# A two-layer attention kernel: whole-tile work moved from GpSimd to VectorE

## The chip, the cores and the metric

The kernel runs on one core of one Trainium2 chip. A core has five engines, each with an instruction queue of its own that it works through in order: TensorE (PE in the profile; its weight loads are listed as PEld), VectorE (DVE), ScalarE (ACT), GpSimd (POOL) and SyncE (SP, which here issues the DMA transfers). The metric is the device time of one launch in microseconds (us), the median of several runs.

## What is computed

Two layers are applied to 256 context tokens and to 1024 latent tokens of width 1024. Both layers norm the tokens, modulate them with a scale and a shift from a conditioning vector, mix the tokens with gated attention, project, norm again and add the result to the stream. Layer 0 uses differential attention (two softmaxes per head, subtracted), layer 1 multi-head latent attention. Cut to what matters:

```python
for i in range(2):
    hc = rmsnorm(x_ctx, g_pre[i]) * (1.0 + sc_c) + sh_c
    hl = rmsnorm(x_lat, g_pre[i]) * (1.0 + sc_l) + sh_l
    if i == 0:                       # 8 heads, q and k in two parts of 64, v of 128
        qc, kc, vc, gc = diff_project(hc, da_w_in[0])
        oc = diff_attend(qc, kc, vc, gc, lam, lam_init, da_g_sub[0])
        ql, kl, vl, gl = diff_project(hl, da_w_in[0])
        ql, kl = apply_rope(ql, *rope_da), apply_rope(kl, *rope_da)
        ol = diff_attend(ql, concat(kl, cache_k), concat(vl, cache_v), gl, ...)
    else:                            # 8 heads on a compressed latent of 256, 64 rotated dims
        qc, ckv_c, kpe_c, gc = mla_project(hc, ...)
        oc = mla_attend(qc, ckv_c, kpe_c, gc, mla_w_kvb[0])
        ql, ckv_l, kpe_l, gl = mla_project(hl, ...)
        ql, kpe_l = mla_rope(ql, kpe_l, *rope_mla)
        ol = mla_attend(ql, concat(ckv_l, cache_ckv), concat(kpe_l, cache_kpe), gl, mla_w_kvb[0])
    x_ctx = x_ctx + gt_c * rmsnorm(oc @ w_out[i], g_post[i])
    x_lat = x_lat + gt_l * rmsnorm(ol @ w_out[i], g_post[i])
# diff_attend: w = softmax(q0 k0) - lam * softmax(q1 k1); o = rmsnorm(w v) * g_sub * 0.2; o * silu(gate)
```

The outputs are both streams and the context tokens' keys, values and latents.

## The kernel before, in words

**Tiling.** Tokens are handled in five pairs of 128-row tiles, four latent pairs (0 to 3) and one context pair (4). Matrix products keep nearly full float32 precision by splitting each operand into a rounded high part and the low rest: `mm3` (L324) issues three matmuls for each product, high by high (L327), high by low (L328) and low by high (L329). So every operand needs a cast (the high part, mostly on ACT) and a subtraction (the low part).

**Where the low parts are made.** `weights` (L304) loads a weight tile `wst` by DMA, casts it on ACT to `wh` (L319) and subtracts to `wl` (L320): on GpSimd, or, where the caller gives `lo_engs=self.LO`, in turn on GpSimd and VectorE. `weights_x` (L347) does the same for the rotated weights on GpSimd (L365). `norm_pair_to_hT` (L280) transposes the normed tokens on PE (L290), applies scale and shift on ACT into `hfull` (L297; three buffers in layer 0, two in layer 1), casts to `hh` on VectorE (L298) and subtracts to `hl` (L299), on VectorE for some of the eight columns and on GpSimd for the others. `yT_load` (L1401) reloads layer 1's head outputs, casts them on ACT (L1407) and subtracts on GpSimd (L1408).

**Stages in order.**
1. Start (0 to about 100 us): modulation vectors, norm of layer 0, the first value projection. `norm_pair` (L256) takes the sums of squares on ACT (L263), adds them (L266), and `rstd` (L248) makes the reciprocal root on GpSimd in two steps (L251 scales and adds epsilon, L253 raises to the power -0.5); VectorE then scales the rows (L270).
2. Queries and keys of layer 0 (to about 330 us), `l0_qk_item` (L374): 32 x 3 matmuls for a half tile, an ACT copy (L421), a rotation in six steps (L427 twice, L428 twice, L429, L430) on GpSimd for queries and on VectorE for keys, then a split into high and low (L385, L386) and a store. Cached and context keys are rearranged on GpSimd (L406, L455).
3. Layer 0's attention (to about 970 us), `l0_heads` (L820): 72 units, nine per head. Each has scores on PE (L603), maxima on VectorE (L605, L612 to L614), exponentials on ACT (L617, L619), the weighted difference on VectorE (L648), transposes on PE (L671), their split on ACT and VectorE (L673, L674), and values on PE. Between these steps a feeder doles out the other projections (values, gates, modulation). After each pair of units `l0_values` (L678) norms the head's output: squares on ACT (L701), `rstd` on GpSimd, then, on GpSimd too, the factor `of` (L706) and the product (L707), and a store to DRAM. `y_chunk` (L743) reloads four heads' outputs two by two with the gate, multiplies them on GpSimd (L757), and PE transposes them (L768).
4. The seam (about 950 to 1150 us): `out_items` (L929) multiplies by the output weights, `residual` (L974) makes the post-norm and adds it to the stream (roots L983 and additions L989, L993 on GpSimd, the rest on VectorE), and layer 1's norm and transposes follow for each pair.
5. Layer 1's projections (to about 1340 us), its attention (`l1_heads` L1332, to about 1870 us) and its output projection with the residual again. Its attention has scores (L1277 to L1281), maxima (L1287, L1289), exponentials (L1295, L1296) and a scaling by the reciprocal sum (L1302).

**What sets the order.** The kernel's text gives a dependency graph and a priority; the framework then draws each engine's queue from it by an estimate of when each operand is ready. Only a stretch of PE at the start is ordered by hand. An engine's queue is therefore not in the order of the text, but once drawn it is fixed: an instruction whose operand is late holds all behind it.

**Buffers around the change.** `wh` and `wl` have five buffers, `wst` three; `ztmp` in `residual` has one; PSUM tiles of the scores have two.

## Time and profile before

| what | us |
|---|---|
| median of 3 runs | 1993.41 (1992.21 to 1994.4) |
| the profiled execution | 1997.65 |
| its span, first to last instruction | 1995.8 |
| granted TensorE clock over the span | 0.989 |

The profile is of one execution. Its page lists busy time of each engine, groups of instructions by line, and for each group what ended the idle time in front of it. "L320 POOL" is line 320 run on GpSimd. `wl<-wst,wh` is output and inputs by the program's tile names. A row of the waits reads "engine, tile and line that waited <- engine, tile and line that released it: us in total, times, longest". In a timeline a row is start, duration, engine, line, operation, and in brackets the idle time before it.

The page's forty slices of 50 us, each digit a busy share in tenths, show the stages:

```
PE   6999999999999999999998999999999999999998
DVE  4644446788878786888427533446667767777413
ACT  4422123667666665666435533335445554455421
POOL 3354443213121212224334442100000000004214
```

PE is nearly full from start to end, VectorE fullest in the two attentions, and GpSimd has work mainly in the first 1200 us and in the last 200.

### The profile page before, as it was taken

To read this page: it belongs to the slowest core of one execution; us is meant where nothing else is said; L and a number is where in the kernel's file an instruction comes from. 1 tells how busy PE (TensorE), PEld (TensorE's weight loads), DVE (VectorE), ACT (ScalarE), POOL (GpSimd) and SP (SyncE) were. 2 spreads that over 40 slices of the span, in tenths; PEclk is the share of its full clock that TensorE was granted. 3 is DMA by queue.
4 is the path that set the end of the run, shared out by engine and by line. 5 is a ranking of instruction groups with operands and counts; after the bars stand their busy time and mean duration, and the time that the engine had idled before them with its cause. 6 is when DMAs were issued, how large, how long until landed. Compare 5 with 4: busy or idle time off the path is not lost.

```text
span 1995.8 us, 36154 instructions
## 1 busy us (share of the span) xinstructions
PE 1911.7 (96%) x13468; PEld 1721.9 (86%) x13468; DVE 1248.4 (63%) x2461; ACT 963.9 (48%) x2409; POOL 498.9 (25%) x693
## 2 busy tenths in 40 slices
PE   6999999999999999999998999999999999999998
PEld 5788888798989787988898999889899999998998
DVE  4644446788878786888427533446667767777413
ACT  4422123667666665666435533335445554455421
POOL 3354443213121212224334442100000000004214
PEclk9999999999999999999998999999999999999999
DMA  8555544544455454455624312442110111113412
GB/s 307 170 169 175 188 157 137 157 138 132 128 147 162 129 165 127 133 148 180 194 98 135 97 51 62 145 135 60 42 36 28 47 39 50 38 38 96 160 56 106
DMA packets 225009, 237.66 MB, mean 119 GB/s; under 512 B 25313, under 2 KB 192577, under 8 KB 224705
## 3 DMA queue, kind: packets, MB, share of 16 engines
q1 hardware_dynamic: 224672, 235.29, 38.3%
q8 instruction: 107, 1.75, 0.4%
q14 instruction: 70, 0.57, 0.1%
q10 hardware_dynamic: 160, 0.05, 0.0%
HBM read 160.48 MB, written 74.78 MB: 118 GB/s over the span
## 4 chain that ended last, share of the span: by engine, by line
PE 43%; DVE 5%; POOL 3%; ACT 2%; issue 2%; DMA 2%; SPq 0%; POOLq 0%; ACTq 0%; DVEq 0%
PE pj L327 7%; PE pj L329 7%; PE pj L328 7%; PE tp L671 3%; PE tp L327 3%; PE tp L328 3%; PE tp L329 3%; PE S L1280 1%; PE S L1281 1%; PE S L1278 1%; PE S L1279 1%; PE S L1277 1%; PE S L603 1%; DVE ptl L674 1%; DMA yst<-yTd 1%
## 5 line engine op out<-in xcount | busy, mean ns | idle before, releaser
L327 PE MATMUL pj<-wh,hh 128*128 128x256 f32 (+1 forms) x1264 | 369.4, 292 | 6.6 <-DVE ptl L674 3.5
L328 PE MATMUL pj<-wl,hh 128*128 128x256 f32 (+1 forms) x1264 | 359.1, 284 | 6.1 <-DVE wl L320 3.7
L329 PE MATMUL pj<-wh,hl 128*128 128x256 f32 (+1 forms) x1264 | 358.8, 284 | 3.4 <-POOL hl L299 1.7
L320 POOL TENSOR_TENSOR wl<-wst,wh 128x512 fp32r<-128x512 f32 (+3 forms) x95 | 110.7, 1173 | 655.1 <-ACT wh L319 608.9
L327 PEld LDWEIGHTS pj<-wh,hh 128*128 128x128 f32 x1264 | 241.7, 191 | 11.7 <-DVE ptl L674 4.1
L328 PEld LDWEIGHTS pj<-wl,hh 128*128 128x128 f32 x1264 | 242.2, 192 | 8.3 <-DVE wl L320 4.1
L329 PEld LDWEIGHTS pj<-wh,hl 128*128 128x128 f32 x1264 | 241.7, 191 | 6.5 <-POOL hl L299 3.1
L329 PE MATMUL pj<-hh,wl 128*128 128x512 f32 (+1 forms) x512 | 188.5, 368 | 1.0 <-POOL wl L365 0.9
L327 PE MATMUL pj<-hh,wh 128*128 128x512 f32 (+1 forms) x512 | 188.3, 368 | 0.0
L328 PE MATMUL pj<-hl,wh 128*128 128x512 f32 (+1 forms) x512 | 187.8, 367 | 0.0
L605 DVE TENSOR_REDUCE mA<-S 128x1 f32<-128x1024 f32 x128 | 155.4, 1219 | 46.8 <-PE S L603 45.9
L617 ACT ACTIVATE e<-S,bias 128x1024 f32<-128x1024 f32 x128 | 142.9, 1117 | 81.6 <-DVE bias L614 81.4
L603 PE MATMUL S<-kl,q 128*128 128x512 f32 x512 | 150.4, 414 | 5.5 <-ACT e L617 5.1
L673 ACT CAST pth<-tp 128x512 fp32r<-128x512 f32 (+1 forms) x208 | 98.4, 511 | 83.0 <-PE tp L671 81.9
L673 ACT CAST pth<-pj 128x512 fp32r<-128x512 f32 (+1 forms) x192 | 98.4, 519 | 73.4 <-PE pj L671 70.8
L674 DVE TENSOR_TENSOR ptl<-tp,pth 128x512 fp32r<-128x512 f32 (+1 forms) x208 | 115.1, 580 | 14.1 <-ACT pth L673 13.3
L648 DVE SCALAR_TENSOR_TENSOR e<-e,cf,e 128x512 f32<-128x512 f32 (+1 forms) x192 | 121.4, 674 | 1.1
L674 DVE TENSOR_TENSOR ptl<-pj,pth 128x512 fp32r<-128x512 f32 (+1 forms) x192 | 113.0, 592 | 12.1 <-ACT pth L673 11.5
L329 PEld LDWEIGHTS pj<-hh,wl 128*128 128x128 f32 x512 | 96.3, 188 | 20.9 <-POOL wl L365 3.9
L328 PEld LDWEIGHTS pj<-hl,wh 128*128 128x128 f32 x512 | 96.3, 188 | 16.9
L319 ACT CAST wh<-wst 128x512 fp32r<-128x512 f32 (+3 forms) x136 | 76.7, 574 | 70.1 <-issue 24.9
L603 PEld LDWEIGHTS S<-kl,q 128*128 128x128 f32 x512 | 88.8, 192 | 25.1 <-ACT e L617 8.1
(323 smaller groups left out, 5247.7 us busy)
## 6 DMA issues: line engine op xcount, KB each, us to landing
q<-qsd SPq DMA_DIRECT2D x320, 64.0 KB, 2.1
wst<-in_da_w_in_dram SPq DMA_DIRECT2D x64, 256.0 KB, 3.5
kl<-ksd SPq DMA_DIRECT2D x64, 192.0 KB, 3.7
wst<-in_w_out_dram SPq DMA_DIRECT2D x48, 256.0 KB, 2.9
ast<-in_w_ada_dram SPq DMA_DIRECT2D x8, 1024.0 KB, 6.3
wh<-in_w_ada_dram SPq DMA_DIRECT2D x32, 256.0 KB, 4.2
wl<-in_w_ada_dram SPq DMA_DIRECT2D x32, 256.0 KB, 5.1
vdh<-s SPq DMA_DIRECT2D x24, 256.0 KB, 2.1
```

Source lines behind the costliest of these rows:

```text
L319: nc.scalar.copy(wh, st)
L320: (lo_engs or [nc.gpsimd])[k0 // kb % len(lo_engs or [0])].tensor_tensor(out=wl, in0=st, in1=f32(wh), op=ALU.subtract)
L327: nc.tensor.matmul(out, a[0], b[0], start=first, stop=False)
L328: nc.tensor.matmul(out, a[0], b[1], start=False, stop=False)
L329: nc.tensor.matmul(out, a[1], b[0], start=False, stop=last)
L603: nc.tensor.matmul(S[:, so:so + 512], st(cc, o), kl[cc][:, so:so + 512], start=(o == 0), stop=(o == 1))
L605: nc.vector.reduce_max(out=mA[:, cc:cc + 1], in_=S, axis=AX.X)
L617: nc.scalar.activation(u.es[cc][:, 0:1024], A[cc], AF.Exp, bias=bias[:, cc:cc + 1], scale=0.125, accum_out=u.zA[:, cc:cc + 1])
L648: nc.vector.scalar_tensor_tensor(out=w[:, sl], in0=w[:, sl], scalar=cf, in1=e0[:, sl], op0=ALU.mult, op1=ALU.add)
L671: nc.tensor.transpose(tp[:, j, :], u.e[:, (c0 + j) * P:(c0 + j + 1) * P], self.ident)
L673: nc.scalar.copy(hi, tp[:, 0:cn, :])
L674: nc.vector.tensor_tensor(out=u.ptl[g][:, 0:cn, u.i * P:(u.i + 1) * P], in0=tp[:, 0:cn, :], in1=f32(hi), op=ALU.subtract)
```

## The change

Each whole-tile operation of GpSimd is issued on VectorE instead. GpSimd keeps the powers (L253, L983) and the constants set up at the start. The factor `of` (L706) is dropped: the product L707 takes both scalars in one instruction. The lists of engines for `weights` go. The kernel's buffers, its loops and the order of its text stay.

```diff
     def rstd(self, pool, ss, n, width=1, tag="rs"):
-        nc.gpsimd.tensor_scalar(out=v, in0=ss, scalar1=1.0 / n, scalar2=EPS, op0=ALU.mult, op1=ALU.add)
+        nc.vector.tensor_scalar(out=v, in0=ss, scalar1=1.0 / n, scalar2=EPS, op0=ALU.mult, op1=ALU.add)
         nc.gpsimd.tensor_tensor(out=r, in0=v, in1=self.mhalf[:, 0:width], op=ALU.pow)
...
-                (nc.vector if k in (self.HL if l else (1, 3, 5, 7)) else nc.gpsimd).tensor_tensor(out=hl[:, k, :], in0=full, in1=f32(hh[:, k, :]),
-                                                              op=ALU.subtract)
+                nc.vector.tensor_tensor(out=hl[:, k, :], in0=full, in1=f32(hh[:, k, :]), op=ALU.subtract)
...
-            (lo_engs or [nc.gpsimd])[k0 // kb % len(lo_engs or [0])].tensor_tensor(out=wl, in0=st, in1=f32(wh), op=ALU.subtract)
+            nc.vector.tensor_tensor(out=wl, in0=st, in1=f32(wh), op=ALU.subtract)
...
-            nc.gpsimd.tensor_tensor(out=vl, in0=sv, in1=f32(vh), op=ALU.subtract)
+            nc.vector.tensor_tensor(out=vl, in0=sv, in1=f32(vh), op=ALU.subtract)
...
-        rot = nc.gpsimd if kind == "q" else nc.vector
...
-                    rot.tensor_tensor(out=m[x], in0=r[x], in1=sin, op=ALU.mult)
-                    rot.tensor_tensor(out=r[x], in0=r[x], in1=cos, op=ALU.mult)
-                rot.tensor_tensor(out=r[0], in0=r[0], in1=m[1], op=ALU.subtract)
-                rot.tensor_tensor(out=r[1], in0=r[1], in1=m[0], op=ALU.add)
+                    nc.vector.tensor_tensor(out=m[x], in0=r[x], in1=sin, op=ALU.mult)
+                    nc.vector.tensor_tensor(out=r[x], in0=r[x], in1=cos, op=ALU.mult)
+                nc.vector.tensor_tensor(out=r[0], in0=r[0], in1=m[1], op=ALU.subtract)
+                nc.vector.tensor_tensor(out=r[1], in0=r[1], in1=m[0], op=ALU.add)
...
         for i in range(2):
-            f = self.t(c.st, [P, 1], "of")
-            nc.gpsimd.tensor_tensor(out=f, in0=r[:, i:i + 1], in1=rz[i], op=ALU.mult)
-            nc.gpsimd.tensor_scalar(out=y[:, i, :], in0=y[:, i, :], scalar1=f, scalar2=None, op0=ALU.mult)
+            nc.vector.tensor_scalar(out=y[:, i, :], in0=y[:, i, :], scalar1=r[:, i:i + 1], scalar2=rz[i],
+                                    op0=ALU.mult, op1=ALU.mult)
...
-        nc.gpsimd.tensor_tensor(out=y, in0=y, in1=g, op=ALU.mult)
+        nc.vector.tensor_tensor(out=y, in0=y, in1=g, op=ALU.mult)
...
-            nc.gpsimd.tensor_tensor(out=xt[:, i, :], in0=xt[:, i, :], in1=tmp, op=ALU.add)
+            nc.vector.tensor_tensor(out=xt[:, i, :], in0=xt[:, i, :], in1=tmp, op=ALU.add)
...
-                nc.gpsimd.tensor_tensor(out=z[:, i, :], in0=z[:, i, :], in1=x0[i], op=ALU.add)
+                nc.vector.tensor_tensor(out=z[:, i, :], in0=z[:, i, :], in1=x0[i], op=ALU.add)
...
-            nc.gpsimd.tensor_tensor(out=lo[:, h, :], in0=st, in1=f32(hi[:, h, :]), op=ALU.subtract)
+            nc.vector.tensor_tensor(out=lo[:, h, :], in0=st, in1=f32(hi[:, h, :]), op=ALU.subtract)
```

In the same way move the rearrangements of keys (L406, L455), the sums of squares (L266, L965) with their scaling (L966), the low part and the rotation of layer 1's rotated keys (L1072, L1093), and all calls of `weights` that named `self.LO`.

More of the change, by code (lines that the diff above doesn't have):

```diff
@@ L265, in norm_pair @@
         if n == 2:
-            nc.gpsimd.tensor_tensor(out=ss[:, 0, :], in0=ss[:, 0, :], in1=ss[:, 1, :], op=ALU.add)
+            nc.vector.tensor_tensor(out=ss[:, 0, :], in0=ss[:, 0, :], in1=ss[:, 1, :], op=ALU.add)
         r = self.rstd(sp, ss[:, 0, :], D, 2)
@@ L405, in gen @@
                 for t in range(2):
-                    nc.gpsimd.tensor_copy(halves[:, t, :].rearrange("p (x g d) -> p x g d", g=4, x=2),
+                    nc.vector.tensor_copy(halves[:, t, :].rearrange("p (x g d) -> p x g d", g=4, x=2),
                                           cr[:, t, :].rearrange("p (g x d) -> p x g d", g=4, x=2))
@@ L964, in gen @@
                             for j in (1, 2):
-                                nc.gpsimd.tensor_tensor(out=ss[:, 0, :], in0=ss[:, 0, :], in1=ss[:, j, :], op=ALU.add)
-                            nc.gpsimd.tensor_scalar(out=ss[:, 0, :], in0=ss[:, 0, :], scalar1=1.0 / D,
+                                nc.vector.tensor_tensor(out=ss[:, 0, :], in0=ss[:, 0, :], in1=ss[:, j, :], op=ALU.add)
+                            nc.vector.tensor_scalar(out=ss[:, 0, :], in0=ss[:, 0, :], scalar1=1.0 / D,
                                                     scalar2=EPS, op0=ALU.mult, op1=ALU.add)
@@ L970, in gen @@
                         yield None
-            return lambda: self.weights(W, [(n * 256, 256)], lo_engs=self.LO), gen
+            return lambda: self.weights(W, [(n * 256, 256)]), gen
         return [item(n, prs) for prs in groups for n in range(4)]
@@ L1016, in gen @@
                     yield None
-        return lambda: self.weights(W, cols, lo_engs=self.LO), gen
+        return lambda: self.weights(W, cols), gen
     def split_T(self, ps, pstag, srcs, out, nb):
@@ L1071, in kp_split @@
             nc.vector.tensor_copy(ks[:, :, 0:3:2, :], kpe.unsqueeze(2).to_broadcast([P, 2, 2, 64]))
-            nc.gpsimd.tensor_tensor(out=ks[:, :, 1, :], in0=kpe, in1=f32(ks[:, :, 0, :]), op=ALU.subtract)
+            nc.vector.tensor_tensor(out=ks[:, :, 1, :], in0=kpe, in1=f32(ks[:, :, 0, :]), op=ALU.subtract)
             def store():
@@ L1092, in ev_q2 @@
             if pr < CTXP:
-                self.rope_inplace(c2.pool, kpe.unsqueeze(2), 2 * pr, 1, nc.gpsimd)
+                self.rope_inplace(c2.pool, kpe.unsqueeze(2), 2 * pr, 1, nc.vector)
             else:
@@ L1129, in gen @@
                         nc.sync.dma_start(self.gTd[h][s + j], g[:, j, :])
-            return lambda: self.weights(W, [(704 + h * P, P)], kb=4, lo_engs=self.LO), gen
+            return lambda: self.weights(W, [(704 + h * P, P)], kb=4), gen
         Wq = I["mla_w_qb"][0].rearrange("(kc p) n -> p kc n", p=P)
@@ L1192, in l1_kn @@
         Wk = I["mla_w_kvb"][0].rearrange("(kc p) n -> p kc n", p=P)
-        wk = self.weights(Wk, [(h * 256, P)], lo_engs=self.LO[::-1] if h == 0 else None)
+        wk = self.weights(Wk, [(h * 256, P)])
         yield 1
@@ L1214, in l1_qn @@
         Wq = I["mla_w_qb"][0].rearrange("(kc p) n -> p kc n", p=P)
-        wq = self.weights(Wq, [(h * 192, P)], lo_engs=self.LO[::-1] if h == 0 else None)
+        wq = self.weights(Wq, [(h * 192, P)])
         yield 1
@@ L1234, in l1_v @@
         Wk = I["mla_w_kvb"][0].rearrange("(kc p) n -> p kc n", p=P)
-        wv = self.weights(Wk, [((h + j) * 256 + P, P) for j in range(2)], lo_engs=self.LO[::-1] if h == 0 else None)
+        wv = self.weights(Wk, [((h + j) * 256 + P, P) for j in range(2)])
         yield 1
```

5 lines of the change are left out of this document (2 added, 3 removed).

## The prediction

> **What bounds the kernel now.** I read the page's busy shares first, then PE's own rows in the view of the waits.
>
> ```profile
> span 1995.8 us, 36154 instructions
> ...
> PE 1911.7 (96%) x13468; PEld 1721.9 (86%) x13468; DVE 1248.4 (63%) x2461; ACT 963.9 (48%) x2409; POOL 498.9 (25%) x693
> ```
>
> TensorE (PE) is busy for 96% of the span, so without touching a matmul no more than 1995.8 - 1911.7 = 84.1 us can be won. What counts is where PE stood still, and behind whom (total us, times, longest):
>
> ```profile
> PE pj L134 <- DMA ast<-in_w_ada_dram: 9.9, 1, 9.9
> PE xt L290 <- ACT hfull L297: 9.8, 5, 3.4
> PE S L603 <- ACT e L617: 5.1, 6, 2.7
> PE pj L327 <- DVE ptl L674: 3.7, 6, 1.3
> PE pj L328 <- DVE wl L320: 3.7, 2, 3.3
> PE pj L768 <- POOL xt L757: 3.3, 1, 3.3
> PE xt L290 <- DVE x L270: 3.2, 3, 1.6
> ...
> PE pj L328 <- POOL wl L320: 2.3, 5, 0.8
> ...
> PE pj L329 <- POOL hl L299: 1.7, 6, 0.3
> ```
>
> The first row is the start-up load, which the change leaves alone. Directly behind GpSimd (POOL) stand 3.3 + 2.3 + 1.7 = 7.3 us; more stands behind VectorE (DVE) and ScalarE (ACT), a part of it POOL at second hand. The view by windows shows which stage has room on DVE; its columns are the stretch and its length, busy PE, PEld, DVE, ACT, POOL, then clock, DMA share and GB/s:
>
> ```profile
> 0.00:100.00 100.00, 80.49 (x569) 66.18 (x570) 54.98 (x119) 42.30 (x81) 35.53 (x51) 0.97 0.72 239
> 100.00:330.00 230.00, 227.41 (x1208) 191.95 (x1208) 105.18 (x138) 50.16 (x98) 111.53 (x93) 0.99 0.52 169
> 330.00:950.00 620.00, 597.82 (x4312) 529.10 (x4312) 505.22 (x991) 404.43 (x1059) 150.08 (x267) 0.99 0.50 145
> 950.00:1150.00 200.00, 182.24 (x1451) 174.18 (x1450) 103.52 (x185) 98.27 (x262) 79.61 (x105) 0.96 0.41 129
> ```
>
> PE stands 19.5 us at the start, 22.2 in layer 0's attention (330 to 950) and 17.8 in the seam between the layers (950 to 1150): 59.5 of the 84.1. In the attention DVE is already 505/620 = 81% busy and POOL does 150 us beside it; there the change can hurt. In the seam DVE is half idle; there it can help.
>
> **What moved work costs, and what it gives back.** Two source views (min/median/max ns) and one row of the groups (busy us, mean ns):
>
> ```profile
> L429 DVE TENSOR_TENSOR r<-r,m x8: 682/684/685, 96.8 to 281.3; 128x512 f32<-128x512 f32 x8
> L429 POOL TENSOR_TENSOR r<-r,m x8: 1284/1294/1302, 129.1 to 311.4; 128x512 f32<-128x512 f32 x8
> ```
>
> ```profile
> L614 DVE SCALAR_TENSOR_TENSOR bias<-m,negl x64: 143/151/1316, 323.4 to 949.4; 128x2 f32<-128x2 f32 x64
> ```
>
> ```profile
> L614 DVE SCALAR_TENSOR_TENSOR bias<-m,negl 128x2 f32<-128x2 f32 x64 | 14.2, 221 | 0.2
> ```
>
> The same rotation step takes 684 ns on DVE and 1294 on POOL. And a DVE instruction that meets POOL is held up: L614, two elements per lane and 151 ns at the median, once took 1316, the length of a whole POOL tile. Its mean gives what that cost on this one step: (221 - 151) x 64 = 4.5 us, directly ahead of the exponentials L617. That comes back, because POOL is left with roots on two columns.
>
> Layer 0's attention, POOL's groups by form within that window:
>
> ```profile
> L707 POOL TENSOR_SCALAR y<-y,of 128x128 f32<-128x128 f32 x76 | 49.1, 658 | 0.0
> L320 POOL TENSOR_TENSOR wl<-wst,wh 128x512 fp32r<-128x512 f32 x24 | 30.9, 1305 | 70.6 <-ACT wh L319 70.2 <-DMA wst<-in_da_w_in_dram 0.4
> L253 POOL TENSOR_TENSOR ors<-orsv,mhalf 128x2 f32<-128x2 f32 x38 | 27.5, 724 | 3.2
> L706 POOL TENSOR_TENSOR of<-ors,rz 128x1 f32<-128x1 f32 x60 | 13.2, 242 | 2.4
> L757 POOL TENSOR_TENSOR kl<-kl 128x512 f32<-128x512 f32 x8 | 10.7, 1334 | 30.5 <-DMA kl<-g 28.7 <-PE pj L694 1.8
> L757 POOL TENSOR_TENSOR wst<-wst,wst 128x512 f32<-128x512 f32 x7 | 9.4, 1349 | 0.3 <-DMA wst<-g 0.2
> L251 POOL TENSOR_SCALAR orsv<-oss 128x2 f32<-128x2 f32 x38 | 7.3, 192 | 371.0 <-ACT oT L701 370.8
> ```
>
> The 24 halves L320 and 15 gate products L757 come to 39 x 0.684 = 26.7 us on DVE, the 38 steps L251 to 38 x 0.151 = 5.7. L706 goes away (the scalar of L707 takes it in). For L707, 128 elements with a scalar per row, the trace has no DVE row. The nearest are L1302's two forms:
>
> ```profile
> L1302 DVE TENSOR_SCALAR e<-e,rz 128x1280 f32<-128x1280 f32 x64 | 56.9, 889 | 1.0
> ...
> L1302 DVE TENSOR_SCALAR e<-e,rz 128x256 f32<-128x256 f32 x16 | 6.3, 393 | 0.5
> ```
>
> Their slope, (889 - 393)/1024 = 0.48 ns per element, gives 393 - 62 = 331 ns; L614's 151 is the lower end, 393 the upper. I take 300, near the row it is closest to: 76 x 0.30 = 22.8 us (11.5 to 29.9). [...] No run here shows this form yet, and the sum goes by the 300.
>
> Together DVE gains 26.7 + 5.7 + 22.8 = 55 us and gets back at least 4.5: net some 50 us, to 555/620 = 90%. As its idle time shrinks from 115 to 65 us, what PE waits for behind DVE and ACT there (L617 5.1, L674 3.7: 8.8 us) should grow, by less than 115/65, since an idle stretch that stays is not always in the way: +5. Against it, small steps are no longer held up: -2. I take **+3 us**; the ends are -9 (all of that waiting gone) and +25 (half of the 50 us reaches PE).
>
> Added waits: L707 on DVE now waits for POOL's root of 724 ns, 38 times; queued behind it are the maxima, the residuals L674 and the weighting L648 of the next unit, for which ACT and PE wait. L757 waits for two loads; POOL waited for those for 28.7 us in the L757 row above, harmlessly; on DVE the softmax stands behind. L320 waits for ACT's cast. The queue places these where it expects the data, so only lateness costs. I count it inside the +25.
>
> End of layer 0's last head, POOL's timeline:
>
> ```profile
> 972.04 0.19 POOL L251 TENSOR_SCALAR orsv<-oss 128x2 f32<-128x2 f32 x1 [1.82 <-ACT oT L701]
> 972.32 0.72 POOL L253 TENSOR_TENSOR ors<-orsv,mhalf 128x2 f32<-128x2 f32 x1
> 973.12 0.34 POOL L706 TENSOR_TENSOR of<-ors,rz 128x1 f32<-128x1 f32 x2
> 973.43 1.19 POOL L707 TENSOR_SCALAR y<-y,of 128x128 f32<-128x128 f32 x2
> ```
>
> From 972.04 to 974.62 this is the way to the last y, whose store and reload end in the 3.3 us of L768. The new way drops L706 (0.31 from start to start) and shortens L707 by 1.19 - 0.60 and L757 by 1.33 - 0.68: 1.5 us off a wait of 3.3. **-1.5** (0 to -3.3; what is late next is the reload itself).
>
> The seam. ACT's waits between 950 and 1150:
>
> ```profile
> ACT hfull L297 <- POOL hl L299: 13.5, 9, 3.3
> ACT wh L319 <- DMA wst<-in_w_out_dram: 9.7, 10, 2.3
> ```
>
> PE waits 9.8 us for hfull, and hfull, with two buffers, waits 13.5 us for POOL's hl; POOL's hl stands in its queue behind whole-tile additions:
>
> ```profile
> 1059.09 1.82 POOL L993 TENSOR_TENSOR z<-z,x 128x768 f32<-128x768 f32 x1 [0.89 <-DVE z L991]
> 1060.87 0.77 POOL L299 TENSOR_TENSOR hl<-hfull,hh 128x256 fp32r<-128x256 f32 x1
> ```
>
> On DVE hl follows its cast directly, but the additions and halves now queue there too. I take a third of 9.8, **-3.5** (-9.8 to +5). The second row shows what an engine in order loses on late loads, about 1 us each; the halves L320 on DVE inherit it.
>
> Start: x L270 3.2 and hl 1.7 behind POOL or its hops, DVE 55% busy: **-2** (-5 to +2). Halves elsewhere (2.3): **-1.5** (0 to -2.3). The rotations (100 to 330) run with PE standing 2.6 us and DVE 46% busy: 0, as the matmuls of the next weight tiles cover them; with that cover gone, each of the eight would show the four dependent steps that its result waits for, some 2 us. The loads L1408 in layer 1's last head go onto a DVE busy with softmax: **+1** (0 to +4). The end:
>
> ```profile
> 1990.02 0.48 DVE L987 SCALAR_TENSOR_TENSOR ztmp<-pj,rs,gp 128x256 f32<-128x256 f32 x1 [0.74 <-POOL rs L983]
> 1990.42 1.01 DVE L995 SCALAR_TENSOR_TENSOR z<-z,rs,x 128x768 f32<-128x768 f32 x1
> 1990.58 1.43 POOL L989 TENSOR_TENSOR x<-x,ztmp 128x256 f32<-128x256 f32 x1 [0.60 <-DVE ztmp L987]
> 1992.03 0.33 SPq L1692 DMA_DIRECT2D out_dram<-x  x1
> ```
>
> POOL's addition runs beside L995; on one engine the two follow each other, and little is won: **-1** (0 to -2).
>
> Sum: +3 - 1.5 - 3.5 - 2 - 1.5 + 1 - 1 = -5.5 us. The profiled execution took 1997.65 us (span plus 1.85), which gives 1992.15; the median of the runs shown, 1993.41, lies 4.24 lower, so I forecast 1993.4 - 5.5 = **1987.9 us**, with 1980 to 1996 as this case's own range.
>
> **Rivals.** *DVE becomes the bound in layer 0's attention.* Place: 330 to 950. Price: half of DVE's 50 us, +25 in place of +3, so 2010. It decides once lateness fills the 65 us left: 38 waits of up to 0.72 and 15 of about 1 come to 42. For it speak the 81%; against it that PE waits only 8.8 us there now. [...]
>
> *All of POOL's second-hand waiting goes:* 9.8 + 3.3 + 3.2 + 2.3 + 1.7 = 20.3 us, and the attention wins its 4.5: -25, so 1969. For it, the 1316 ns of L614; against it, that the work stays and DVE does it in the same order.
>
> *Nothing:* the seams' 9.5 us and the attention's loss cancel: 1993.
>
> **How the numbers follow.** About 0.2% (4 us) is what a measurement here tells from no change. Forecast 0.50 (faster 0.30, same 0.20), DVE bound 0.26 (slower), large gain 0.14 (faster), nothing 0.10 (same): faster 0.44, same 0.30, slower 0.26. The range, 1971 to 2008, cuts the far ends of both outer rivals.
>
> **What would show it.** Right: no DVE instruction of two columns over 0.8 us; hfull no longer behind POOL; DVE near 555 us in 330 to 950; PE's standing in 330 to 950 within 5 us of 22. Wrong: DVE idle before L707 or L757 with PE waiting behind L614 or L674 in that stage, which is the first rival; PE's standing there falling to half, which is the second.

## The result, and the profile after

The changed kernel takes 1971.36 us (median of 5 runs, 1963.3 to 1972.98) against 1993.42 us, a ratio of 0.9871 with the 95% interval 0.9849 to 0.9894. The forecast was 1987.9 us, a gain of 5.5: the sign was right and the gain at least four times as large, 22 us by the medians and 26 by the ratio. The time lies outside the 1980 to 1996 that the prediction calls this case's own range, and 0.4 us inside the wider one, 1971 to 2008, near the 1969 us of the rival "All of POOL's second-hand waiting goes".

The profiled execution of the changed kernel took 1963.3 us, the fastest of the five, at a granted clock of 0.996. Its page begins:

```profile
span 1961.5 us, 35893 instructions
...
PE 1892.0 (96%) x13468; PEld 1712.6 (87%) x13468; DVE 1330.3 (68%) x2983; ACT 964.3 (49%) x2409; POOL 59.5 (3%) x91
```

GpSimd's busy time fell from 498.9 to 59.5 us. VectorE took over 522 instructions and is busy only 81.9 us longer. The 13468 matmuls of TensorE are the same, yet their busy time is 19.7 us lower; that surprise is taken up below. The windows used for the prediction (busy PE, PEld, DVE, ACT, POOL, then clock, DMA share, GB/s) now read:

```profile
0.00:100.00 100.00, 83.72 (x587) 69.55 (x588) 55.13 (x157) 43.18 (x82) 5.55 (x15) 0.97 0.73 247
100.00:330.00 230.00, 230.00 (x1266) 197.49 (x1265) 131.21 (x243) 55.41 (x110) 0.00 (x0) 1.00 0.53 173
330.00:950.00 620.00, 595.27 (x4331) 526.82 (x4329) 532.91 (x1159) 410.46 (x1072) 31.27 (x39) 1.00 0.50 148
950.00:1150.00 200.00, 190.15 (x1620) 187.05 (x1621) 114.09 (x293) 96.08 (x259) 13.31 (x21) 1.00 0.37 118
```

In the window of layer 0's attention TensorE stands 24.7 us where it stood 22.2; in the seam 9.9 where it stood 17.8, with 169 more matmuls done in the same 200 us; in the q/k stage (100 to 330) it no longer stands at all. The clock column is 1.00 in all but the first window. The windows are cut at the same times in both kernels and hold partly other work, since the changed kernel is 19 us ahead by layer 0's last score. Cut at the same work, by the marks of the table further down, TensorE stands 22.2 us before and 21.0 after from layer 0's first score to its last, and 17.4 before and 7.3 after in the three rows of the seam. TensorE's waits after the change:

```profile
...
PE pj L325 <- DVE ptl L671: 7.6, 12, 1.3
PE xt L289 <- DVE x L269: 4.6, 4, 1.7
PE xt L289 <- ACT hfull L296: 4.4, 4, 2.7
PE S L600 <- ACT e L614: 3.6, 4, 2.5
...
PE pj L326 <- DVE wl L318: 2.3, 2, 1.5
...
PE pj L764 <- DVE xt L753: 1.5, 1, 1.5
```

The wait for hfull is down from 9.8 to 4.4 us and the longest wait for wl from 3.3 to 1.5. The waits for ptl behind a fuller VectorE doubled, from 3.7 to 7.6, but in twelve pieces of at most 1.3 us.

**What became of VectorE's instructions.** Five groups by line and form (busy us, mean ns, then idle time before), first from the kernel before, then from the changed one:

```profile
L386 DVE TENSOR_TENSOR lo<-r,hi 128x512 fp32r<-128x512 f32 x32 | 33.9, 1080 | 0.6
...
L320 DVE TENSOR_TENSOR wl<-wst,wh 128x512 fp32r<-128x512 f32 x37 | 32.1, 872 | 25.4 <-ACT wh L319 25.4
L298 DVE CAST hh<-hfull 128x256 fp32r<-128x256 f32 x80 | 31.0, 398 | 11.7 <-ACT hfull L297 11.3
L385 DVE CAST hi<-r 128x512 fp32r<-128x512 f32 x32 | 30.1, 963 | 68.6 <-POOL r L429 68.6
L299 DVE TENSOR_TENSOR hl<-hfull,hh 128x256 fp32r<-128x256 f32 x50 | 29.6, 595 | 1.4
```

```profile
L318 DVE TENSOR_TENSOR wl<-wst,wh 128x512 fp32r<-128x512 f32 x108 | 73.3, 688 | 33.5 <-ACT wh L317 32.8
...
L298 DVE TENSOR_TENSOR hl<-hfull,hh 128x256 fp32r<-128x256 f32 x80 | 32.7, 421 | 1.2
...
L297 DVE CAST hh<-hfull 128x256 fp32r<-128x256 f32 x80 | 22.2, 288 | 6.8 <-ACT hfull L296 6.5
...
L383 DVE TENSOR_TENSOR lo<-r,hi 128x512 fp32r<-128x512 f32 x32 | 20.6, 684 | 0.0
...
L382 DVE CAST hi<-r 128x512 fp32r<-128x512 f32 x32 | 12.1, 420 | 0.0
```

The same instruction on the same shape is shorter after the change: 1080 ns became 684, 872 became 688, 398 became 288, 963 became 420, 595 became 421. On the instructions that VectorE already had, that is (1080 - 684) x 32 + (872 - 688) x 37 + (398 - 288) x 80 + (963 - 420) x 32 + (595 - 421) x 50 = 12.7 + 6.8 + 8.8 + 17.4 + 8.7 = 54 us of VectorE's time, in five groups.

The two traces also give the whole of it. If each of the 2461 instructions that VectorE had before is set against the mean of its own form after the change, they took 97 us longer in all. The excess lies in the 650 that overlap in time with an instruction of GpSimd (97.8 us); the other 1811 together differ by -0.6 us. By stage it is 13.5 us up to the first q/k product, 32.0 from there to the first score, 18.3 to layer 0's last score, 21.1 to the end of the seam and 12.3 after it.

The two-column step that the prediction used as its sign, and the scaling that moved, by their lines:

```profile
L611 DVE SCALAR_TENSOR_TENSOR bias<-m,negl x64: 148/154/165, 313.5 to 932.1; 128x2 f32<-128x2 f32 x64
```

```profile
L702 DVE TENSOR_SCALAR y<-y,ors,rz x64: 336/343/350, 348.8 to 958.7; 128x128 f32<-128x128 f32 x64
```

The maximum of L611 (L614 before) fell from 1316 to 165 ns.

**Where the time went.** The span cut at marks in TensorE's work that every kernel here has (start of the first q/k product, first and last score, last transpose of layer 0's heads, first and last transpose of layer 1's norm, last transpose of the compressed queries), in us, each from one profiled execution:

| stretch up to | before | changed | only_start | only_qk | start_and_qk | only_seam | whole_ghost |
|---|---|---|---|---|---|---|---|
| first q/k product | 81.3 | 74.9 | 75.2 | 77.7 | 74.8 | 80.0 | 77.3 |
| first score | 236.9 | 234.3 | 240.5 | 234.0 | 234.9 | 235.4 | 239.8 |
| last score of layer 0 | 627.8 | 617.9 | 626.8 | 622.4 | 629.4 | 629.0 | 620.6 |
| last transpose of its heads | 45.2 | 48.0 | 45.1 | 45.6 | 45.7 | 47.2 | 46.8 |
| first transpose of layer 1's norm | 64.0 | 59.0 | 64.1 | 64.2 | 63.0 | 59.0 | 59.0 |
| last one | 84.9 | 75.6 | 85.1 | 85.3 | 86.8 | 77.2 | 82.9 |
| last of the queries' | 81.2 | 78.8 | 81.2 | 81.3 | 81.2 | 79.2 | 82.7 |
| end | 774.6 | 773.1 | 773.2 | 776.9 | 776.4 | 775.7 | 775.0 |

Of the 34.3 us between the two profiled spans, 16.7 come from the three rows of the seam, 9.0 from the first two rows, 9.9 from the attention and 1.5 from the end, less 2.8 in the row of the heads' last transposes. These are single executions. Of the first row's 6.4 us some 2 belong to the start-up load, which TensorE awaited for 9.9 us in the trace of before and for 7.3 to 9.4 us in all others. The attention's row lies between 617.9 and 621.6 us in the six traces of kernels with its work moved, and between 622.4 and 631.7 in the fourteen others.

### The profile page after: what moved, and what is told of

Its sections match the earlier page's. It is cut to its first block, busy times and chain, and to the rows that moved or that the text cites. A ratio compares the mean times of both kernels' runs of the same rounds, so it can differ in the third digit from the quotient of the medians.

```text
span 1961.5 us, 35893 instructions
## 1 busy us (share of the span) xinstructions
PE 1892.0 (96%) x13468; PEld 1712.6 (87%) x13468; DVE 1330.3 (68%) x2983; ACT 964.3 (49%) x2409; POOL 59.5 (3%) x91
## 4 chain that ended last, share of the span: by engine, by line
PE 79%; DVE 11%; DMA 3%; ACT 3%; issue 2%; POOL 1%; SPq 0%; POOLq 0%; ACTq 0%; DVEq 0%
PE pj L325 16%; PE pj L327 16%; PE pj L326 16%; PE S L600 5%; PE tp L668 3%; PE tp L325 3%; PE tp L326 3%; PE tp L327 3%; DVE mA L602 2%; PE pj L668 2%; DVE ptl L671 2%; PE S L1274 1%; PE S L1276 1%; PE S L1277 1%; PE S L1275 1%
## 5 line engine op out<-in xcount | busy, mean ns | idle before, releaser
L614 ACT ACTIVATE e<-S,bias 128x1024 f32<-128x1024 f32 x128 | 143.0, 1117 | 80.9 <-DVE bias L611 80.6
L671 DVE TENSOR_TENSOR ptl<-tp,pth 128x512 fp32r<-128x512 f32 (+1 forms) x208 | 115.3, 582 | 12.3 <-ACT pth L670 11.5
L318 DVE TENSOR_TENSOR wl<-wst,wh 128x512 fp32r<-128x512 f32 (+3 forms) x136 | 84.2, 629 | 41.2 <-ACT wh L317 40.4
L325 PEld LDWEIGHTS pj<-hh,wh 128*128 128x128 f32 x512 | 96.4, 188 | 16.8
L1291 ACT ACTIVATE e<-S,bias 128x1024 f32<-128x1024 f32 x64 | 71.5, 1118 | 76.4 <-DVE bias L1289 69.9
```

Source lines behind the costliest of these rows:

```text
L318: nc.vector.tensor_tensor(out=wl, in0=st, in1=f32(wh), op=ALU.subtract)
L325: nc.tensor.matmul(out, a[0], b[0], start=first, stop=False)
L614: nc.scalar.activation(u.es[cc][:, 0:1024], A[cc], AF.Exp, bias=bias[:, cc:cc + 1], scale=0.125, accum_out=u.zA[:, cc:cc + 1])
L671: nc.vector.tensor_tensor(out=u.ptl[g][:, 0:cn, u.i * P:(u.i + 1) * P], in0=tp[:, 0:cn, :], in1=f32(hi), op=ALU.subtract)
L1291: nc.scalar.activation(e[:, 0:nm], S, AF.Exp, bias=bias, scale=sc, accum_out=Z[:, 0:1])
```

## The experiments

All ratios are to the kernel before on the same chip; us are the ratio times that kernel's median, with the 95% interval behind them.

### One stage at a time

Four kernels take over the change for one stage each. From the kernel before, with the lines of its text:

```diff
 only_start: L251 of layer 0's norm, L299 with l == 0, the first weights of L320
-    nc.gpsimd.tensor_tensor(out=hl[:, k, :], in0=full, in1=f32(hh[:, k, :]), op=ALU.subtract)
+    nc.vector.tensor_tensor(out=hl[:, k, :], in0=full, in1=f32(hh[:, k, :]), op=ALU.subtract)
 only_qk: L365, L427 to L430 for queries, L406, L455
-        rot = nc.gpsimd if kind == "q" else nc.vector
+        rot = nc.vector
 only_attention: L251 of the heads, L706 and L707 as one, L757, the attention's weights of L320
-            nc.gpsimd.tensor_scalar(out=y[:, i, :], in0=y[:, i, :], scalar1=f, scalar2=None, op0=ALU.mult)
+            nc.vector.tensor_scalar(out=y[:, i, :], in0=y[:, i, :], scalar1=r[:, i:i + 1], scalar2=rz[i], ...)
 only_seam: L965, L966, L989, L993, L251 and L266 of layer 1's norms, L299 with l == 1, the seam's weights of L320, L1072, L1093
-            nc.gpsimd.tensor_tensor(out=xt[:, i, :], in0=xt[:, i, :], in1=tmp, op=ALU.add)
+            nc.vector.tensor_tensor(out=xt[:, i, :], in0=xt[:, i, :], in1=tmp, op=ALU.add)
```

> The kernel before with only the start moved to VectorE: the low parts hl of layer 0's norm, the scaling step of its root, and the low parts of the first value weights. The start of the two profiles differs by 6.4 us (81.3 to 74.9 us until the first query matmul), so if the moved work of a stage makes that stage's gain, this kernel is 4 to 8 us faster than before. If instead the gain is one of the whole kernel, from VectorE being free of GpSimd everywhere, it is under 2 us.

> Only the queries and keys of layer 0 moved: the low parts of the rotated weights, the query rotations, the rearrangements of keys. Here TensorE stands 2.9 us in the profile of before and 0.0 in that of after, and VectorE wins back the most time that GpSimd had held it up. Theory that only waits of TensorE count: 2 to 3 us faster. Theory that VectorE's own time counts: more than 8 us faster.

> Only layer 0's attention moved: the scaling step of the head norm's root, the product L707 without the factor of L706, the gate products L757, and the low parts of the value and gate weights. The stage is 7.2 us shorter after, but 6.4 of these are half-speed clock that the profile of before happened to have there. Theory that the work as such is neutral here: 0 to 4 us faster. Rival that VectorE free of GpSimd speeds the softmax: 7 to 12 us faster. Rival of the prediction, VectorE as the bound: slower.

> Only the seam between the layers and what shares its code moved: the residual's additions, the sums and scaling steps of both norms, the low parts hl of layer 1's norm, the low parts of the output and layer 1 projection weights, and the split and rotation of layer 1's rotated keys. The seam is 16.6 us shorter in the profile of after, of which 6.8 are half-speed clock. If TensorE's waits there and the clock that falls behind them make most of the gain: 10 to 16 us faster, with the granted clock of the run up by 0.002 or more. If the gain is spread by VectorE's time: under 6 us.

| kernel | median us | ratio, interval | us |
|---|---|---|---|
| only_start | 1994.01 | 1.0005 [0.9993, 1.0016] | +1 (-1 to +3) |
| only_qk | 1989.2 | 0.9976 [0.9966, 0.9985] | -5 (-7 to -3) |
| only_attention | 1993.95 | 0.9996 [0.9987, 1.0006] | -1 (-3 to +1) |
| only_seam | 1983.07 | 0.9941 [0.9925, 0.9958] | -12 (-15 to -8) |

The seam is the largest part, q/k second, attention neutral. The start is a miss: its stretch became 6.1 us shorter (81.3 to 75.2) and the next one 3.6 us longer (236.9 to 240.5), and no gain was left in the median. The 5 us of q/k lie between its two expectations (2 to 3, and more than 8), so neither TensorE's waits there nor VectorE's whole time gives the size. The four add up to 17 us of the 26. They do not cover the whole change: layer 1's gate and head weights, the rotated weights L365 of its queries and L1408 are in none of the four, and were not run alone.

The framework draws every queue anew for each kernel, so a better order of TensorE's matmuls would be another explanation. Compared place by place, by tile names and shapes, TensorE's queue differs from that of the kernel before in 1199 of 13468 places in only_attention, which gains nothing that shows, but in 28 in only_qk, 182 in only_seam and 202 in seam_and_qk (below), which gain 5, 12 and 21 us. The gain does not follow the amount of reordering. In the whole change 1546 places differ.

### The seam taken apart

My first theory was the buffer: hl on GpSimd frees one of two hfull tiles late. The rivals were the queue (what stands ahead of hl on GpSimd is late) and contention (GpSimd's work slows VectorE's).

```diff
 seam_halves: only L299 in layer 1;  seam_others: all of only_seam but that
-                (nc.vector if k in (self.HL if l else (1, 3, 5, 7)) else nc.gpsimd).tensor_tensor(out=hl[:, k, :], ...
+                (nc.vector if l or k in (1, 3, 5, 7) else nc.gpsimd).tensor_tensor(out=hl[:, k, :], ...
 seam_ghost: only_seam, and after that subtraction in layer 1
+                if l and k not in self.HL:
+                    nc.gpsimd.tensor_tensor(out=self.t(pool, [P, 256], "ghost", bufs=1), in0=f32(hh[:, k, :]),
+                                            in1=f32(hh[:, k, :]), op=ALU.subtract)
 hfull3: the kernel before
-                full = self.t(pool, [P, 256], "hfull", bufs=3 - l)
+                full = self.t(pool, [P, 256], "hfull", bufs=3)
```

> The kernel before, with only the lower halves of the layer-1 norm (blocks 0 and 4 of each pair, the one use of GpSimd at L299 in layer 1) on VectorE. Buffer theory: GpSimd's subtraction of 1.9 us frees the second hfull tile late, TensorE stands behind it and then runs a window at half the clock; so this edit alone gives 5 to 9 us of the 11 of the whole seam, the stretch from the first to the last layer-1-norm transpose falls from 84.9 us to 75-78, and the half-speed window in it goes. Queue theory (the work behind it on GpSimd's queue, residual sums and weights, is what is late): under 2 us faster.

> The seam's other GpSimd work on VectorE (residual sums, mean squares, lower halves of the weights, the k-rope parts), the layer-1 norm's lower halves left on GpSimd. Buffer theory: 2 to 5 us faster, all of it ahead of the first layer-1-norm transpose (64.0 us to about 59), the 84.9 us stretch within 2 us of what it was. Queue theory: 7 to 11 us faster, with both stretches shorter.

> The kernel with the whole seam on VectorE, and a subtraction of the same size back on GpSimd for blocks 0 and 4 of each pair, which reads the upper half and writes a scratch tile that nothing reads; it frees no hfull buffer. Buffer theory: TensorE's gain stays, 9 to 13 us faster than before and within 2 us of the seam alone. Contention theory (GpSimd at work slows or holds VectorE, and that is what the seam had lost): half of the gain or more goes again, 0 to 6 us faster than before.

> The kernel before, every operation on its old engine, but with three hfull tiles in layer 1 instead of two. Buffer theory: the waits of TensorE and ScalarE for hfull shrink without VectorE taking anything over: 3 to 8 us faster, the 84.9 us stretch at 77-82. Contention theory or queue theory: within 2 us of before.

| kernel | median us | ratio, interval | us |
|---|---|---|---|
| seam_halves | 1995.55 | 0.9999 [0.9986, 1.0011] | 0 (-3 to +2) |
| seam_others | 1984.17 | 0.9948 [0.9931, 0.9965] | -10 (-14 to -7) |
| seam_ghost | 1984.47 | 0.9951 [0.9932, 0.997] | -10 (-14 to -6) |
| hfull3 | 1990.51 | 0.9982 [0.9968, 0.9996] | -4 (-6 to -1) |

The buffer theory, by which hl is late because GpSimd makes it, falls with the first row: 5 to 9 us had been expected of it. Nor does the trace of before show the 1.9 us that the expectation gives GpSimd's subtraction: layer 1's ten took 0.73 us at the median and 1.03 at most. In seam_halves GpSimd no longer frees any of layer 1's hfull tiles, and TensorE waits for hfull as before (9.8 us then):

```profile
PE xt L294 <- ACT hfull L301: 10.1, 5, 3.9
```

The wait is named after hfull, but what is late stands further back: in this trace ScalarE still waits 12.2 us in the seam for a free hfull tile, now behind VectorE's hl. A third buffer helps a little by itself (7.4 us of TensorE's wait are left in its trace). Its 4 us are what the buffer theory expected (3 to 8); a spare tile would bridge lateness of any cause, which was not tried apart. seam_ghost keeps 10 us, within the 9 to 13 of the buffer theory and not the 0 to 6 of contention. Its ten subtractions are 9.6 us of GpSimd's time, little beside the moved work, so a larger ghost follows below.

The timeline shows what is late. In the kernel before, shortly ahead of layer 1's first transposes (start us, duration us, engine, line; in brackets the idle time before it):

```profile
1044.64 0.48 DVE L987 SCALAR_TENSOR_TENSOR ztmp<-pj,rs,gp 128x256 f32<-128x256 f32 x1 [0.63 <-POOL xt L989]
...
1045.05 1.62 DVE L270 TENSOR_SCALAR z<-z,rs 128x768 f32<-128x768 f32 x2
...
1046.55 1.26 POOL L320 TENSOR_TENSOR wl<-wst,wh 128x512 fp32r<-128x512 f32 x1 [0.30 <-ACT wh L319]
1046.58 2.05 DVE L995 SCALAR_TENSOR_TENSOR z<-z,rs,x 128x768 f32<-128x768 f32 x1
1048.55 1.28 DVE L320 TENSOR_TENSOR wl<-wst,wh 128x512 fp32r<-128x512 f32 x2
```

VectorE first waits 0.63 us for GpSimd's sum, because ztmp has one buffer. Then L995 takes 2.05 us, as GpSimd started its wl 0.03 us ahead of it; behind it on VectorE's queue stand the two wl for which TensorE waits 3.3 us. After the change the same step takes 1.01 and the wait is 1.48:

```profile
1028.23 1.01 DVE L991 SCALAR_TENSOR_TENSOR z<-z,rs,x 128x768 f32<-128x768 f32 x1
...
1029.16 0.48 DVE L983 SCALAR_TENSOR_TENSOR ztmp<-pj,rs,gp 128x256 f32<-128x256 f32 x1
...
1029.56 0.68 DVE L318 TENSOR_TENSOR wl<-wst,wh 128x512 fp32r<-128x512 f32 x1
...
1030.29 0.39 PE L326 MATMUL pj<-wl,hh 128*128 128x256 f32 x1 [1.48 <-DVE wl L318]
```

So both a hand-over (the sum) and a hold-up (the wl beside L995) are in the way. The next runs took them one at a time and together.

```diff
 seam_sums: L989 and L993
-            nc.gpsimd.tensor_tensor(out=xt[:, i, :], in0=xt[:, i, :], in1=tmp, op=ALU.add)
+            nc.vector.tensor_tensor(out=xt[:, i, :], in0=xt[:, i, :], in1=tmp, op=ALU.add)
 seam_weights: L320 for the output projection and layer 1's token projection
-            return lambda: self.weights(W, [(n * 256, 256)], lo_engs=self.LO), gen
+            return lambda: self.weights(W, [(n * 256, 256)], lo_engs=[nc.vector]), gen
 seam_sums_weights: both
```

> The kernel before with only the residual sums (the two additions on whole tiles per tile of tokens, L989 and L993) on VectorE. Hand-over theory: each sum costs a trip VectorE to GpSimd and back (VectorE's next ztmp waited 0.63 us for GpSimd's sum), and that ladder is what is late; then this part alone gives 5 to 9 us of the seam's 11, with TensorE's 3.3 us wait for wl and the half-speed window behind it gone. Hold-up theory (GpSimd's halves of the weights and other whole tiles hold VectorE's instructions beside them): 0 to 4 us.

> The kernel before with only the lower halves of the seam's weights that GpSimd made (every other one at L320 for the output projection and the layer-1 token projection) on VectorE. Hold-up theory: the z row of 2.05 us beside GpSimd's wl goes back to 1.01, the weights are not late: 5 to 9 us faster. Hand-over theory: VectorE takes 1.3 us per two more and the ladder of the sums stays, so between 3 us slower and 2 us faster.

> Only the residual sums and the seam's weights on VectorE. Alone they gave 5 and 1 us, the seam without the lower halves 10. If the two pay only together (the sums' ladder and the z rows held beside GpSimd's wl are late in turn): 8 to 11 us faster. If the remaining small rows (mean squares, k-rope parts, two columns each) carry the rest, as GpSimd's queue is then free for the reciprocal roots: 4 to 7 us faster.

| kernel | median us | ratio, interval | us |
|---|---|---|---|
| seam_sums | 1990.35 | 0.9976 [0.9967, 0.9985] | -5 (-7 to -3) |
| seam_weights | 1995.57 | 0.9996 [0.9985, 1.0006] | -1 (-3 to +1) |
| seam_sums_weights | 1986.44 | 0.9952 [0.9939, 0.9964] | -10 (-12 to -7) |

The two together give nearly all of the seam, and more than one by one (10 against 6, with intervals that overlap a little). The traces agree. Between 940 and 1150 us TensorE waits for ScalarE's hfull and VectorE's wl together 13.5 us in the kernel before, 10.9 with the sums moved, 13.6 with the weights and 8.4 with both: with one of two delays gone, TensorE still waits for the other.

### Stages together

> Seam and the q/k stage on VectorE, the rest as before. If the parts add, 15 to 18 us faster (11 and 5 alone). If the whole change's 22 to 26 us comes from these two together, by TensorE keeping its clock over more of the span, 20 us or more.

> The whole change without the output scaling, the gate product and the weights of layer 0's attention, which stay on GpSimd as before. If attention is neutral, as alone, within 3 us of the whole change (20 to 26 us faster). If its move pays only beside the others (the second-hand waiting of the small VectorE steps), 14 to 18 us faster. If it costs there, more than 27 us faster, and this version beats both.

> The start (lower halves of the layer-0 norm, mean squares, first weights) and the q/k stage on VectorE, the rest as before. The start alone gave nothing: its stretch was 6 us shorter in the profile and the q/k stretch behind it 3.6 longer. Theory that GpSimd's rotations and rearrangements in the q/k stage took the start's gain back: 8 to 11 us faster than before, with the first stretch at about 75 us and the second at about 234. Theory that the start is worth nothing: 4 to 6 us faster, as q/k alone.

| kernel | median us | ratio, interval | us |
|---|---|---|---|
| seam_and_qk | 1974.39 | 0.9895 [0.9882, 0.9908] | -21 (-24 to -18) |
| all_but_attention | 1973.5 | 0.9891 [0.9876, 0.9905] | -22 (-25 to -19) |
| start_and_qk | 1989.1 | 0.9963 [0.9949, 0.9977] | -7 (-10 to -5) |

seam_and_qk and start_and_qk are sums of edits shown above. all_but_attention is the whole change without the edits of only_attention, and so has layer 1's weights and L1408 too. seam_and_qk gives more than its parts (12 + 5), though the intervals meet. start_and_qk keeps both short stretches (74.8 and 234.9), as the theory of a gain given back wanted, and the median shows about 2 us more than q/k alone, less than expected; its other stretches were longer in that execution. all_but_attention is level with seam_and_qk and within the uncertainty of the whole change: moving the attention's work adds between nothing and a few us, and the start and layer 1's work add nothing that shows beside the seam and q/k.

### GpSimd's work without its results

The question that decides: is it GpSimd's working at all that costs? whole_ghost is the whole change with 290 GpSimd instructions added that read upper halves and write scratch tiles.

```diff
 norm_pair_to_hT, for the blocks that GpSimd had
+                    for o in (0, P):
+                        nc.gpsimd.tensor_tensor(out=<scratch 128x128>, in0=f32(hh[:, k, o:o + P]), in1=f32(hh[:, k, o:o + P]), ...
 weights, in the seam, where lo_engs named GpSimd
+                for o in range(0, kn * tot, P):
+                    nc.gpsimd.tensor_tensor(out=<scratch 128x128>, in0=gv[:, o:o + P], in1=gv[:, o:o + P], op=ALU.subtract)
 put, for queries
+                for o in [0, n // 2] * 3:
+                    nc.gpsimd.tensor_tensor(out=<scratch 128x256>, in0=f32(hi[:, o:o + n // 2]), in1=f32(hi[:, o:o + n // 2]), ...
 whole_hfull3: the whole change, and
-                full = self.t(pool, [P, 256], "hfull", bufs=3 - l)
+                full = self.t(pool, [P, 256], "hfull", bufs=3)
```

> The whole change, and on GpSimd again subtractions of the old sizes into scratch tiles that nothing reads: for the lower halves of both norms, for the seam's weights and in place of the q rotations (not for the other weights, the residual sums and the rearrangements). Hold-up theory (GpSimd's work itself slows VectorE beside it): half or more of the 22 us is lost, 5 to 12 us faster than before. Hand-over theory (only results that came late from GpSimd cost): 17 to 24 us faster.

> The whole change with three hfull tiles in layer 1 instead of two. If the hfull waits that are left in the seam (4.4 us of TensorE) are for the tile: 2 to 4 us faster than the whole change, 24 to 29 faster than before, and so ahead of both kernels. If VectorE's pace sets them: the same as the whole change within 2 us.

whole_ghost took 1986.84 us, ratio 0.9957 [0.9943, 0.9971]: 9 us faster than before (6 to 11) where the change itself is 26. Two thirds of the gain are gone, and the other queues are nearly the same: in the two traces the 13468 matmuls and the 2409 instructions of ScalarE follow each other in the same order, VectorE has the same 2983 instructions with 17 places of its queue filled differently, and no other engine waits for a ghost. The ghosts' rows, with the empty list of who waited:

```profile
L403 POOL TENSOR_TENSOR ghost<-hi x144: 400/664/968, 127.9 to 327.3; 128x256 bf16<-128x256 f32 x96, 128x128 bf16<-128x128 f32 x48
L308 POOL TENSOR_TENSOR ghost<-hh x60: 400/462/1045, 20.2 to 1126.8; 128x128 bf16<-128x128 f32 x60
...
who waited for it (us, times):
```

```profile
L334 POOL TENSOR_TENSOR wghost<-wh x86: 400/408/2463, 967.3 to 1173.0; 128x128 bf16<-128x128 f32 x86
...
who waited for it (us, times):
```

The page and the groups of whole_ghost:

```profile
PE 1904.4 (96%) x13468; PEld 1721.5 (87%) x13468; DVE 1370.7 (69%) x2983; ACT 966.6 (49%) x2409; POOL 243.0 (12%) x381
```

```profile
L330 DVE TENSOR_TENSOR wl<-wst,wh 128x512 fp32r<-128x512 f32 x108 | 76.2, 717 | 33.7 <-ACT wh L328 32.7
...
L304 DVE TENSOR_TENSOR hl<-hfull,hh 128x256 fp32r<-128x256 f32 x80 | 38.6, 495 | 1.2
...
L406 DVE TENSOR_TENSOR lo<-r,hi 128x512 fp32r<-128x512 f32 x32 | 27.9, 910 | 0.0
L303 DVE CAST hh<-hfull 128x256 fp32r<-128x256 f32 x80 | 27.4, 355 | 6.2 <-ACT hfull L302 6.0
```

VectorE's same instructions take 40.4 us longer (1370.7 - 1330.3), in the groups that run beside a ghost above all: lo from 684 to 910 ns, hl from 421 to 495, hh from 288 to 355. Set against their forms after the change, the 345 that overlap an instruction of GpSimd hold 40.3 us of it. The windows put it where the ghosts are:

```profile
100.00:330.00 230.00, 226.26 (x1221) 192.28 (x1220) 149.86 (x232) 49.94 (x97) 101.74 (x144) 1.00 0.51 168
330.00:950.00 620.00, 596.49 (x4332) 528.88 (x4332) 532.20 (x1154) 410.34 (x1072) 30.65 (x38) 1.00 0.51 148
950.00:1150.00 200.00, 182.97 (x1487) 178.29 (x1486) 122.03 (x278) 99.22 (x262) 72.55 (x124) 0.96 0.39 124
```

In q/k TensorE stands 3.7 us again (0 after the change), in the three rows of the seam, cut at the marks of the table, 11.8 (7.3 after, 17.4 before); in the attention, where no ghost was put, DVE and PE are as after the change. That GpSimd's work itself holds VectorE up is thus shown, and that this work costs the changed kernel some 17 us (26 - 9). It is not shown that two thirds of the gain came this way: in whole_ghost VectorE does the moved work besides, and its stretch to the first score (239.8 us) is longer than that of the kernel before (236.9). Nor is all of it standing. The two profiled spans differ by 22.6 us, 10.2 of them standing and 12.4 longer busy time of the same matmuls; half the length of the half-speed stretches (next section) is 20.1 us in the one trace and 8.6 in the other. By what means GpSimd's work holds VectorE's instructions up, no run here shows; measured is only how much, as in the 2.05 us of L995 beside a 1.26 us wl, where it takes 1.01 after the change.

whole_hfull3 took 1969.52 us, ratio 0.9868 [0.9852, 0.9884], the same as the change within the uncertainty. The third tile gives nothing once the lateness is gone.

### Waits of two lengths

In the traces, 78 of the 116 stretches in which TensorE runs at half its clock come with its waits of 2 us or more (counted below). In the kernel before, around the wait of 3.3 us for wl:

```profile
1040.00:1044.00 4.00, 4.00 (x37) 4.00 (x36) 2.08 (x5) 0.72 (x4) 2.43 (x5) 1.00 0.97 321
1044.00:1048.00 4.00, 1.20 (x9) 0.81 (x7) 3.37 (x5) 2.88 (x7) 2.91 (x3) 0.98 0.44 164
1048.00:1055.00 7.00, 5.71 (x28) 5.72 (x29) 4.12 (x9) 3.55 (x11) 2.28 (x5) 0.53 0.72 224
```

Ahead of the wait 37 matmuls go in 4.00 us. Behind it the granted clock is 0.53 and 28 matmuls keep TensorE busy for 5.71 us. Over all 20 traces, between 90 and 1950 us, TensorE's waits of 0.8 us and more, and how many had a half-speed stretch begin between their start and 4 us after their end (a short wait near a long one counts too):

| wait, us | 0.8 to 1.5 | 1.5 to 2 | 2 to 2.5 | 2.5 to 3 | 3 to 3.5 | over 3.5 |
|---|---|---|---|---|---|---|
| waits | 272 | 27 | 33 | 35 | 21 | 11 |
| with half speed | 29 | 8 | 23 | 27 | 17 | 11 |

Counted from the wait's end on, the second row is 28, 8, 18, 18, 6 and 2: in most of the longest waits the clock falls while TensorE still stands. Nor is a long wait needed. Of the 116 half-speed stretches there, 78 come with a wait of 2 us or more by this count, and 38 with shorter ones alone, as in the kernel before at 317 us behind two waits of 1.6 us together. In that part of the span the profiled execution of the kernel before has seven such stretches (five of 3.4 us and two of 6.8, at a granted clock of 0.50), that of the changed kernel one (3.4 us). To try it, waits were put into the whole change:

```diff
+    def stand(self, pj, pool, n):      # called in out_items of layer 1, ahead of a tile's products
+        d = self.t(pool, [P, P], "stand", bufs=1)
+        pt = self.t(pj, [P, 2, 256], "pj")
+        nc.tensor.transpose(pt[:, 0, 0:P], self.ident, self.ident)
+        nc.vector.tensor_copy(d, pt[:, 0, 0:P])
+        for _ in range(n):             # stand_long: 16, four calls; stand_short: 1, sixteen calls
+            nc.vector.tensor_scalar(out=d, in0=d, scalar1=1.0, scalar2=None, op0=ALU.mult)
+        nc.tensor.transpose(pt[:, 1, 0:P], d, self.ident)
```

> The whole change, and in the closing projection (the last 112.6 us of TensorE, no wait in any kernel so far) four added waits: TensorE turns a tile, VectorE copies it and goes over it 16 times, TensorE turns the result; some 3 to 5 us of standing each, 12 to 20 in all, as the trace will show. If a wait costs its length, the closing part grows by what TensorE stands there plus the 8 transposes, and no half-speed stretch shows in it. If a long wait drops the clock, each one has a half-speed stretch of 3.4 to 6.8 us behind it, and the part grows by 1.7 to 3.4 us a wait more than it stands: 7 to 14 us.

> The same with 16 added waits of one pass each, about 1 us of standing each, 12 to 20 us in all. By the length of the wait alone the kernel is as much slower than the whole change as with four long ones. If only long waits drop the clock, no half-speed stretch shows, and the part grows by what TensorE stands alone.

stand_long took 1977.3 us, 0.99 [0.9884, 0.9917]; stand_short 1976.11 us, 0.9901 [0.9885, 0.9917]. The long waits did not arise, since the framework put other matmuls into them. stand_long's trace:

```profile
PE pj L993 <- DVE stand L992: 4.5, 4, 1.8
```

No wait is over 1.8 us and no half-speed stretch follows; the closing part grew by 6.3 us in stand_long (4.6 of it standing) and by 7.0 in stand_short (0.7 standing, the rest the 32 turns, 0.2 us each). With eight turns at that price stand_long's part comes to 4.6 + 1.6 = 6.2 us, so these four waits of up to 1.8 us cost about their length. That a long one costs more by itself is only read from the traces, not tried.

## Why the prediction was off

**The step that failed is the hold-up in the sum.** The prediction saw that "a DVE instruction that meets POOL is held up" and priced it from one row, L614, at 4.5 us, in the attention alone. Over all of VectorE's instructions it was 97 us (above): 32.0 in q/k, 21.1 from the end of the attention through the seam and 13.5 in the start, where no term counted it, and 18.3 in the attention. whole_ghost shows that hold-up of this kind moves TensorE (its standing went from 0 to 3.7 us in q/k and from 7.3 to 11.8 in the seam). In the seam the hand-over of the sums, which had no term either, came with it.

**Term by term.**
- Attention, +3 (-9 to +25): alone -1 (-3 to +1), and TensorE's standing from first to last score went from 22.2 to 21.0. The forecast was 4 us off. VectorE rose to 532.9 us in the window, not to 555, although L702 took 343 ns instead of 300 (the slope of L1302's forms gave 331). The shortfall is hold-up that went: 18.3 us by the count above, where 4.5 were taken off.
- End of layer 0's last head, -1.5: the wait L768 did fall from 3.3 to 1.5 us, but the stretch did not (45.2 to 48.0, in a single execution). No gain shows.
- Seam, -3.5 (-9.8 to +5): alone -12 (-15 to -8). This is the term with the largest error. It was a third of the wait for hfull, by the buffer that hl frees late, and that mechanism fell with seam_halves: what counted were the sums and the weights, as hand-over and hold-up.
- Start, -2: nothing alone; its stretch did shrink by 6.1 us, some 2 of them the start-up load, and 3.6 were given back in the next.
- Halves elsewhere, -1.5, and the rotations, 0: q/k alone gave 5 (3 to 7). The matmuls did not cover all of it: the stretch from first product to first score went from 236.9 to 234.0, and the one ahead from 81.3 to 77.7.
- Layer 1's attention, +1, and the end, -1: the last row of the stretches is 1.5 us shorter in all. Right within what can be told.

**A second thing had no term: the clock.** "Without touching a matmul no more than 84.1 us can be won" took TensorE's busy time as fixed. It fell by 19.7 us with the same matmuls, a part of it as half-speed stretches went: half their length is 22.8 us in the trace of before and 8.6 in that of after, which is the fastest of its five runs. The runs of the kernel before show what is usual: in the 104 beside the experiments the median was 2000.29 us at a granted clock of 0.987 (4 runs), 1996.6 at 0.989 (21), 1993.87 at 0.991 (24) and 1992.62 at 0.992 (14). The changed kernel's five ran at 0.991 to 0.996, and the two at 0.995 and 0.996 took the least time (1965.56 and 1963.3). Over those 104 runs the share of the span lost to the clock averages 20.5 us, over the changed kernel's five 13.8: about 7 of the 26 us, an estimate from clocks that are given to three digits. It is not a cause apart from the waits as far as these runs tell.

**The signs.** No two-column step over 0.8 us, hfull no longer behind POOL, TensorE's standing in the attention within 5 us of 22: these came as written, though ScalarE still waits 10.2 us in the seam for hfull, now behind VectorE's hl (13.5 before). VectorE near 555 us did not. Of the rivals, "DVE becomes the bound" failed: there is room left at 533 of 620 us, and the added waits are short. The large gain has nearly the right size, in part by luck. It counted waits behind GpSimd and not VectorE's lengthened instructions, and of those waits hfull went from 9.8 to 4.4 and L768 from 3.3 to 1.5, while the one for x grew from 3.2 to 4.6. Its sign, TensorE's standing in the attention falling to half, did not come.

**What stays open.** The four parts alone sum to 17 us and the whole gives 26. Seam with q/k gives more together than apart, which accounts for much of it; whether the rest is the attention's move (shorter in every trace that has it, without a gain alone), the start's gain kept, layer 1's weights or the clock is within the intervals. How the gain divides between hold-up and hand-over was not measured. And a long wait's own price was not tried.

## What to carry to other kernels

Before giving GpSimd a share of the elementwise work, compare VectorE's mean for one form with its minimum: where the mean is far above it (here 1080 against 681 ns for lo) and GpSimd is busy at the time, multiply the difference by the count, and set that against what GpSimd takes over. To tell a late result from contention, leave the results where they are and put back the engine's work on scratch tiles. When a wait has two causes in one queue, taking away one may show little (here 5 and 1 us, against 10 for both), so try them together before dropping one. And compare stages between marks in the work, not between fixed times.
